# A constant tile of a transformer-layer kernel made 64 bytes larger, so that everything laid out behind it moves by 64 bytes

## The chip, the core and the metric

The kernel runs on one core of one Trainium2 chip. The time is in microseconds of device time for one execution, the median of several runs. The core has a matrix engine (TensorE, "PE" in the profile, with its weight loads shown apart as "PEld"), VectorE ("DVE"), ScalarE ("ACT"), GpSimd ("POOL") and SyncE ("SP"), which here issues the DMAs. Data lives on the chip in SBUF, 128 partitions with one address range that all partitions share; a tile takes the same byte range in every partition. Matmul results go to PSUM.

## The reference

One layer of a streaming encoder, for 512 tokens of width 2048, in fp32:

```
mod = silu(c) @ w_ada + b_ada                        # six vectors: sh1 sc1 g1 sh2 sc2 g2
h = rms_norm(x, norm1_g) * (1 + sc1) + sh1
proj = h @ w_in                                      # 8 gated-recurrence heads and 8 attention heads of 128
mixed = concat(hgrn2(...), stick_breaking(...)) @ w_out
x = x + g1 * mixed
h = rms_norm(x, norm2_g) * (1 + sc2) + sh2
gate, up = split(h @ w_ffn_in)                       # 2048 -> 2 * 5632
x = x + g2 * ((silu(gate) * up) @ w_ffn_out)         # 5632 -> 2048
```

## The kernel before

All of it is one function, `trunk`. The projections are kept at fp32 accuracy by splitting each operand in two parts, a rounded one (`hi`, type float32r) and the rest (`lo`), and summing three matmuls: hi by hi, hi by lo, lo by hi. A weight block comes in by DMA into one of four `raw` buffers; `split` (lines 211 to 222) then has ScalarE write its `hi` part (line 220) and VectorE its `lo` part (line 221). There are three `hi` and three `lo` buffers, used in turn.

The stages, in order: a first product with the raw `x` (tiles `st`), the projections of the attention heads (`sbp`, 384 columns a matmul) with the attention itself beside them, those of the recurrence heads (`hgf`, `hgq`, `hgg`, 512 columns), the output projection (`wo`, 512 columns), the first feed-forward product (`ffA`, `ffB`, `ffC`, 256 columns) and the second (`foA`, `foB`, `foC`, 512 columns). The rows of the modulation `w_ada` are multiplied on VectorE in between (line 180).

In every one of these matmuls one operand is stationary: it is loaded into the array as 128 columns of 4 bytes, 512 bytes of each partition. The other is moving: 256, 384 or 512 columns stream past. Both are read from SBUF.

The first feed-forward product is the longest stage. It does 42 turns `f`, from 2 to 43; each has seven block products (a scheme that needs seven products where eight are usual), named by their weights `ff_1` to `ff_7`. A product is 24 matmuls: 8 blocks of the contraction, for each of which the `hi` weights meet the `hi` and the `lo` part of the activations and the `lo` weights meet the `hi` part. The weights are stationary; the activations `opA`, `opD`, `opB`, `opC` are moving. In this stage `split` takes, at every fourth call, a spare pair of buffers in place of the usual three (lines 214 to 215): `hi2` and `lo2`, allocated in the pool `tp` on the right-hand side. The profile calls weights in the spare pair `ff_1hi`, `ff_1lo` and so on, with an i or an o behind, and weights in the usual buffers `ff_1h`, `ff_1l`. In the last stage every fourth call takes a pair inside the place of `hlo` instead, on the left.

**The layout.** SBUF is given out from both ends. Pools on the left side begin at low addresses and follow one another in the order in which they are opened: `const`, `wp` (raw, hi, lo), `hp` (the two large operand tiles `hhi` and `hlo`, whose place `opB` and `opC` take later), then the pools of the stages. Pools with `side="right"` are laid from the top downwards: `x` and `x1`, later `tp` and `rp` (with the spare pair), later `T2` and `O`. A slot is rounded up to a multiple of 32 bytes. `lead`, the tile of the diff, holds two partial sums of the first modulation row; of its columns only the first two are ever used (lines 291 and 293). It is the fifth tile of `const`, behind `cond`, `small`, `ones` and `epsb`.

The places that follow from this, as bytes from the start of a partition, and what is left of each over a multiple of 256:

| tile | side | byte | over a multiple of 256 |
|---|---|---|---|
| `cond`, `ones`, ahead of `lead` | left | 384, 9216 | 128, 0 |
| raw buffers | left | 11040, 19232, 27424, 35616 | 32 |
| hi buffers | left | 43808, 47904, 52000 | 32 |
| lo buffers | left | 56096, 60192, 64288 | 32 |
| `hhi`, later `opB` | left | 68384 | 32 |
| `hlo`, later `opC` | left | 101152 | 32 |
| `opA` (later `opsA`), `opD` | left | 133920, 166688 | 32 |
| spare pair `hi2`, `lo2` | right | 213984, 218080 | 224 |

Blocks inside these tiles are 512 bytes or a multiple of it apart, so that every operand of a matmul begins as far over a multiple of 256 as its tile does.

Of the kernel before, what the change touches and what calls it, by code (L numbers as in the profile page):

```python
# [10 lines left out]
F32 = mybir.dt.float32  # L11
# [6 lines left out]
P = 128  # L18
# [111 lines left out]
def trunk(ctx, tc, a):  # L130
# [5 lines left out]
    const = ctx.enter_context(tc.tile_pool(name="const", bufs=1))  # L136
# [20 lines left out]
    one = ones[:, 0:1]  # L157
    epsb = const.tile([P, 1], F32, name="epsb")
    G.memset(epsb, EPS)
    lead = const.tile([P, 2], F32, name="lead")  # L160
    left = [KT] * 6
    mod = const.tile([P, 96], F32, name="mod")
    gain1 = const.tile([P, KT], F32, name="gain1")
# [1179 lines left out]
```

## Time and profile before

| | |
|---|---|
| median of 3 runs | 2311.63 us (2308.95 to 2312.49) |
| the profiled execution | 2309.45 us, of which the span of the instructions is 2307.6 us |
| PE busy | 2253.1 us, 98% of the span |
| PEld busy | 2049.8 us, 89% |
| DVE busy | 1919.5 us, 83% |
| ACT busy | 1160.1 us, 50% |
| DMA queue | 53.0% of 16 engines' time, 435.42 MB |
| mean granted clock of TensorE | 0.995 |

The profile comes from one execution. A row of a group gives the source line, the engine, the operation, output and inputs, the shapes, the count, then the busy time in us and the mean of one in ns. Nearly all matmuls stand at line 93, in a helper. A matmul's own duration is longer than the distance from one matmul to the next, since several are in flight; the cost of one in a stream is read from the distance between starts. The chain of waits follows the work that ended last, from the last instruction back.

### The profile page before, as it was taken

Reading aid. Unit: us, or ns where it says so; the run is one execution under the profiler, and the core shown is the slowest. Engines: PE = TensorE matmul, PEld = TensorE weight load, DVE = VectorE, ACT = ScalarE, POOL = GpSimd, SP = SyncE. Lnnn points to the kernel's source line nnn. Section 1 sums busy time; section 2 is a strip of 40 time slices with the busy share of each in tenths; the row PEclk is TensorE's granted clock in tenths of the full one; section 3 lists DMA queues with packets and bytes.
Section 4 is the critical chain, followed back from the end, with each engine's and each line's share of the span. In section 5 each row is a group of like instructions: output and inputs, shape, how many; then the busy total and the mean of one; then the engine's idle time right before and its main releaser. Section 6 shows DMA issues by size and latency. Waiting matters only on the chain.

```text
span 2307.6 us, 35720 instructions
## 1 busy us (share of the span) xinstructions
PE 2253.1 (98%) x14171; PEld 2049.8 (89%) x14171; DVE 1919.5 (83%) x2570; ACT 1160.1 (50%) x2011; POOL 10.7 (0%) x25
## 2 busy tenths in 40 slices
PE   8999899999999999989999999999999999999998
PEld 6899799888888788989999999999999978878776
DVE  8887779999887864699899988888888777888888
ACT  4326666565656422654445444454545545454443
POOL 0000000000000000000000000000000000000000
PEclk9999999999999999999999999999999999999999
DMA  9886446843322486336555534454544486654553
GB/s 368 314 319 225 166 153 230 305 170 126 110 92 76 155 294 209 111 114 238 206 203 197 209 133 165 142 174 142 174 142 157 177 343 237 219 178 142 183 204 87
DMA packets 114978, 437.69 MB, mean 190 GB/s; under 512 B 9822, under 2 KB 58236, under 8 KB 76796
## 3 DMA queue, kind: packets, MB, share of 16 engines
q1 hardware_dynamic: 114812, 435.42, 53.0%
q8 instruction: 111, 1.82, 0.3%
q14 instruction: 55, 0.45, 0.1%
HBM read 386.61 MB, written 48.77 MB: 189 GB/s over the span
## 4 chain that ended last, share of the span: by engine, by line
PE 79%; DVE 11%; DMA 4%; ACT 3%; issue 3%; SPq 0%; DVEq 0%; ACTq 0%
PE ffA L93 17%; PE ffC L93 9%; PE foA L93 8%; PE sbp L93 8%; PE wo L93 7%; PE ffB L93 4%; PE foC L93 4%; PE st L93 4%; PE hgf L93 4%; PE hgq L93 3%; PE hgg L93 3%; PE foB L93 1%; DVE ada L180 1%; PE l L93 1%; DMA opd<-fhi 1%
## 5 line engine op out<-in xcount | busy, mean ns | idle before, releaser
L180 DVE SCALAR_TENSOR_TENSOR ada<-ada,cond 128x2048 f32<-128x2048 f32 x95 | 216.9, 2286 | 49.0 <-DMA ada<-in_w_ada 49.0
L93 PE MATMUL ffA<-opD,ff_3h 128*128 128x256 f32 x512 | 93.6, 283 | 0.8 <-ACT u L1008 0.8
L93 PE MATMUL ffA<-opB,ff_6h 128*128 128x256 f32 x512 | 93.6, 283 | 0.2 <-ACT a L1008 0.2
L93 PE MATMUL ffC<-opB,ff_7h 128*128 128x256 f32 x512 | 93.5, 283 | 0.0
L93 PE MATMUL ffC<-opC,ff_4h 128*128 128x256 f32 x496 | 90.8, 284 | 0.4 <-ACT c L1008 0.3
L93 PE MATMUL ffB<-opA,ff_2h 128*128 128x256 f32 x496 | 91.3, 284 | 0.0
L93 PE MATMUL ffA<-opC,ff_5h 128*128 128x256 f32 x496 | 90.6, 283 | 0.0
L93 PE MATMUL ffA<-opA,ff_1h 128*128 128x256 f32 x496 | 90.6, 283 | 0.0
L1082 ACT CAST fhi<-forms 128x512 fp32r<-128x512 f32 (+1 forms) x63 | 43.6, 692 | 90.6 <-DMA opd<-fhi 74.1
L93 PEld LDWEIGHTS ffA<-opD,ff_3h 128*128 128x128 f32 x512 | 79.8, 192 | 1.0 <-ACT u L1008 1.0
L93 PEld LDWEIGHTS ffA<-opB,ff_6h 128*128 128x128 f32 x512 | 79.7, 192 | 0.4 <-ACT a L1008 0.4
L93 PEld LDWEIGHTS ffC<-opB,ff_7h 128*128 128x128 f32 x512 | 79.8, 192 | 0.0
L93 PEld LDWEIGHTS ffC<-opC,ff_4h 128*128 128x128 f32 x496 | 77.2, 192 | 0.8 <-ACT c L1008 0.8
L93 PEld LDWEIGHTS ffB<-opA,ff_2h 128*128 128x128 f32 x496 | 77.7, 193 | 0.1
L93 PEld LDWEIGHTS ffA<-opC,ff_5h 128*128 128x128 f32 x496 | 77.3, 192 | 0.0
L93 PEld LDWEIGHTS ffA<-opA,ff_1h 128*128 128x128 f32 x496 | 77.3, 192 | 0.0
L1083 DVE TENSOR_TENSOR forms<-forms,fhi 128x512 fp32r<-128x512 f32 (+1 forms) x63 | 49.0, 778 | 31.0 <-ACT fhi L1082 30.6
L93 PE MATMUL ffA<-opD,ff_3l 128*128 128x256 f32 x256 | 72.5, 283 | 0.0
L93 PE MATMUL ffC<-opB,ff_7l 128*128 128x256 f32 x256 | 72.4, 283 | 0.0
L93 PE MATMUL ffA<-opB,ff_6l 128*128 128x256 f32 x256 | 72.4, 283 | 0.0
L93 PE MATMUL ffB<-opA,ff_2l 128*128 128x256 f32 x248 | 70.3, 284 | 0.0
L93 PE MATMUL ffA<-opA,ff_1l 128*128 128x256 f32 x248 | 70.2, 283 | 0.0
(1644 smaller groups left out, 7759.3 us busy)
## 6 DMA issues: line engine op xcount, KB each, us to landing
ada<-in_w_ada SPq DMA_DIRECT2D x95, 1024.0 KB, 5.0
wfo<-in_w_fo SPq DMA_DIRECT2D x16, 1024.0 KB, 6.0
yraw<-in_w_fo SPq DMA_DIRECT2D x16, 1024.0 KB, 5.1
fix<-in_w_fix SPq DMA_DIRECT2D x14, 1024.0 KB, 5.7
opsA<-opd SPq DMA_DIRECT2D x12, 1024.0 KB, 4.9
opd<-forms SPq DMA_DIRECT2D x44, 256.0 KB, 3.7
opd<-fhi SPq DMA_DIRECT2D x42, 256.0 KB, 4.2
opd<-forms SPq DMA_DIRECT2D x22, 384.0 KB, 6.7
```

The source lines that it names most:

```text
L93: self.engine.matmul(out, lhsT, rhs, **kw)
L180: V.scalar_tensor_tensor(w, w, 1.0, row, op0=ALU.mult, op1=ALU.mult, accum_out=col)
L1082: S.copy(hi, R[:, q])
L1083: V.tensor_sub(R[:, q].bitcast(F32R), R[:, q], hi.bitcast(F32))
```

## The change

The tile `lead` gets 18 columns in place of 2. It takes 96 bytes a partition in place of 32.

```
-    lead = const.tile([P, 2], F32, name="lead")
+    lead = const.tile([P, 18], F32, name="lead")
```

Nothing else is edited. The program has the same instructions on every engine, in the same order and with the same waits. Each tile on the left side behind `lead` begins 64 bytes higher: raw, hi, lo, `hhi`, `hlo` and the operands are 96 bytes over a multiple of 256, where they were 32. The tiles ahead of `lead`, all tiles on the right side, with the spare pair among them, PSUM and HBM are where they were.

## The prediction

> **What bounds the kernel now.** I read the page first, then the groups of instructions, then a table of stretches, and last the chain of waits in order of time. The page's busy times and the shares of the chain:
>
> ```profile
> PE 2253.1 (98%) x14171; PEld 2049.8 (89%) x14171; DVE 1919.5 (83%) x2570; ACT 1160.1 (50%) x2011; POOL 10.7 (0%) x25
> ...
> PE 79%; DVE 11%; DMA 4%; ACT 3%; issue 3%; SPq 0%; DVEq 0%; ACTq 0%
> ```
>
> TensorE is busy for 98% of the span and makes 79% of the chain, so the time is mostly a count of matmuls times what one costs in a stream. A change that moves no instruction can only act through the length of single operations, and it must act on matmuls to be seen. So I ask whether any operation's length depends on where its operands lie, and this program holds a test of that: in the first feed-forward stage most weights lie in the left buffers, one product in four in the spare pair on the right. The groups:
>
> ```profile
> L93 PE MATMUL ffC<-opB,ff_7h 128*128 128x256 f32 x512 | 93.5, 283 | 0.0
> ...
> L93 PE MATMUL ffA<-opA,ff_1hi 128*128 128x256 f32 x176 | 32.7, 288 | 6.2 <-ACT sg L1104 6.2
> L93 PE MATMUL ffA<-opC,ff_5hi 128*128 128x256 f32 x176 | 30.5, 276 | 0.0
> ...
> L93 PE MATMUL ffC<-opB,ff_7hi 128*128 128x256 f32 x160 | 27.7, 276 | 0.0
> ```
>
> The same shape with the same moving tile `opB` takes 283 ns with left weights and 276 ns with spare ones. (The 288 of `ff_1hi` holds a first wait.) In the chain of waits, in a stretch where PE is never stopped, the distance itself is seen. A turn of `f` runs 1, 2, 6, 7, 5, 4, 3, and columns are start, length, work:
>
> ```profile
> 1230.45 5.60 PE ffA L93 x48
> 1236.05 2.88 PE ffB L93 x24
> 1238.93 2.88 PE ffA L93 x24
> 1241.81 2.72 PE ffC L93 x24
> 1244.53 2.88 PE ffA L93 x24
> 1247.41 2.88 PE ffC L93 x24
> ```
>
> A product of 24 matmuls takes 2.88 us, 120.0 ns for each, or 2.72 us, 113.3 ns each, once in four (the 5.60 is one of either kind). The changes from one to the other fall on the spare products:
>
> ```profile
> 1173.37 0.28 PE L93 MATMUL ffA<-opD,ff_3l 128*128 128x256 f32 x1
> 1173.49 0.39 PE L93 MATMUL ffA<-opA,ff_1hi 128*128 128x256 f32 x2
> ...
> 1176.21 0.40 PE L93 MATMUL ffB<-opA,ff_2h 128*128 128x256 f32 x2
> ```
>
> `ff_1` from the spare pair lasts from 1173.49 to 1176.21, 2.72 us. So the length of a matmul does depend on where its weights lie, by 6.7 ns. Nothing else in those two products differs: `ff_1hi` and the `ff_2h` that follows it both stream `opA`.
>
> **What the 6.7 ns look like.** Three widths of the same kind of matmul, all with left operands on both sides:
>
> ```profile
> 423.41 4.16 PE sbp L93 x24
> ...
> 1855.96 5.44 PE foA L93 x24
> ```
>
> 384 columns take 173.3 ns, 512 take 226.7 ns, 256 take 120.0. Each step of 128 columns adds 53.3 ns, 0.417 ns a column, so that 256 columns alone are 106.7 ns. What is left over is 13.3 ns at all three widths with left weights, and 6.7 ns with spare weights. A fixed extra that does not grow with the width belongs to an event that happens once per matmul, and 6.7 ns are 16 columns, or 64 bytes of a partition. That is the size of a unit in which both operands could be fetched, and it is also the size of the shift.
>
> **The change part by part.** VectorE and ScalarE first. The same split, into the spare pair and into a left buffer:
>
> ```profile
> L220 ACT CAST ff_1hi<-wg10r x1: 1047/1047/1047, 1165.0 to 1165.0; 128x1024 fp32r<-128x1024 f32 x1
> L221 DVE TENSOR_TENSOR ff_1lo<-wg10r,ff_1hi x1: 1226/1226/1226, 1166.1 to 1166.1; 128x1024 fp32r<-128x1024 f32 x1
> ...
> L220 ACT CAST ff_1h<-wg11r x1: 1052/1052/1052, 1185.0 to 1185.0; 128x1024 fp32r<-128x1024 f32 x1
> L221 DVE TENSOR_TENSOR ff_1l<-wg11r,ff_1h x1: 1224/1224/1224, 1186.1 to 1186.1; 128x1024 fp32r<-128x1024 f32 x1
> ```
>
> 1047 against 1052 and 1226 against 1224 ns: neither engine cares. I cost them at nothing; with VectorE at 83% and ScalarE at 50% there is room besides. The wider `lead` itself costs nothing, since the same two columns are written and read.
>
> DMAs next. They make 4% of the chain, 92 us. All loads of weights go to the left side and keep their size; I cost them at nothing, and even 1% on all of these would be 0.9 us either way. [...]
>
> The matmuls carry the sum. For them the position of the operands can count in two ways, by itself or against the other operand. Look at the distances. Left weights and left moving tiles lie a multiple of 256 bytes apart, before and after, since both shift. The spare pair lies 224 over a multiple of 256 and the moving tiles 32: they are 192 apart modulo 256, an odd number of 64-byte units. After the change the moving tiles are at 96, and the distance is 128, an even number of units, like the left weights' distance of nothing. **If what matters is whether weights and moving operand run through the same half of a 128-byte pattern at the same time**, all the rows above follow: left against left meets once in each matmul, waits one unit of 16 columns (6.7 ns), and then runs out of step, so that the price is the same at every width; spare against left never meets. I take this as likeliest because the extra is one unit, occurs once, and does not depend on the width. Counting the units that the weights touch explains nothing: 512 bytes from 32 and 512 bytes from 224 cross equally many boundaries of 64, 128 or 256 bytes.
>
> What follows is a loss, and only for the spare products, which would go from 2.72 to 2.88 us. Their number comes from the seven groups of `hi` weights in the spare pair, of which the first, the third and the last stand above: four with 176 matmuls and three with 160 are 1184, and at 16 a product that is 74 products. 74 times 0.16 us is 11.8 us. How much of it reaches the end depends on whether PE sets the pace:
>
> ```profile
> 1005.00:1150.00 145.00, 139.90 (x1152) 139.25 (x1152) 135.06 (x154) 71.36 (x105) 0.00 (x0) 0.98 0.55 195
> 1150.00:1845.00 695.00, 693.99 (x5859) 693.59 (x5860) 587.06 (x662) 348.59 (x509) 0.00 (x0) 1.00 0.48 168
> ```
>
> (Columns: stretch, its length, busy us of PE, PEld, DVE, ACT, POOL, clock, DMA share, GB/s.) From 1150 to 1845 PE is busy for 693.99 of 695 us, and every lost ns counts: 35 turns with 7/4 spare products each are 61, or 9.8 us. From 1005 to 1150 PE has 5 us idle and the chain runs through DMAs and VectorE; the other 13 products cost between nothing and 2.1 us there. I take 1.2, a bit over half, as PE is still 96% busy: 11.0 us in all, with bounds of 9.8 and 11.8. All other stages keep their distance of nothing and their times. Sum against the profiled execution's own time, 2309.45 us (span 2307.6 and 1.85 around it): 2309.45 + 11.0 = **2320.5 us**. That execution lies 2.2 us under the median of 2311.63; with that and the bounds the likeliest case spans 2318 to 2325.
>
> **Rivals.** *No change.* What sets the 6.7 ns may be something that the shift leaves alone: the region (the spare pair lies above 208 thousand bytes, all left weights below 69 thousand), or a pattern longer than 128 bytes, in which the new distance of 128 is as good as 192. For it: all rows fix only one fast and one slow case. Against it: the extra of just 16 columns points to a short pattern, and weights at 68384 (`hhi`, in the `sbp` row above) or 133920 (`opsA`, in the `foA` row above) cost the same 13.3 ns as those at 43808, so region does not show among them. Time: 2309.5 to 2312, the profiled execution to the median. [...]
>
> *Faster.* The weights' position may count by itself. Modulo 128 the spare pair stands at 96 and left tiles at 32; after the change all left tiles stand at 96 too. If a start at 96 is what saves 6.7 ns, the other 220 of the 294 products gain 0.16 us each: 35 us, 2274. If matmuls of other stages gain as well, there are 1536 of 384 columns, 4104 of 512 and 480 more of 256 in the program, at 6.7 ns some 41 us more, 2233; but there VectorE and DMAs make part of the chain, and I take 60 us in all, 2249. VectorE would not stop the gain in the long stage: 587 us of busy time fit in 695 − 29. For it: one and the same position fits the fast rows. Against it: no count of boundaries tells 32 from 96. It decides if absolute position rules, whatever the distance.
>
> *Much slower.* A start at 96 for the moving operands may cost a second 6.7 ns everywhere: 13176 matmuls in the program, 88 us, 2397. No row shows a moving operand elsewhere than at 32, so it can't be excluded.
>
> **How the numbers follow.** Likeliest case 0.36, no change 0.34, faster 0.25 (most of it with all stages), much slower 0.05. The forecast is 2320.5 us. No two of the first three can be left out of a range that should hold 8 times in 10, so it goes from 2242, under the faster case at 2249, to 2326, over the likeliest one's top. About 0.2%, 4.6 us, is what a measurement of this kernel can tell from no change. Faster 0.25, same 0.34, slower 0.41.
>
> **What would show it.** In the profile after, groups `ff_1hi` to `ff_7hi` at 283 ns and no 2.72 left in the chain: the likeliest case. Those at 276 and `ff_7h` at 283: no change. `ff_7h` at 276 and `foA` under 5.44: faster. If `ff_7h` or `foA` grow, the moving operand counts by itself. In each case VectorE's 1.22 us and ScalarE's 1.05 us should stay; if they move, the argument is wrong at its first step.

## The result, and the profile after

| | before | after |
|---|---|---|
| median | 2311.63 us (2308.95 to 2312.49, 5 runs) | 2318.41 us (2314.87 to 2321.05, 5 runs) |
| ratio to before | | 1.0035, 95% interval 1.0024 to 1.0045 |
| span of the profiled execution | 2307.6 us | 2316.3 us |
| long stage (first `ffA` matmul to first `foB` matmul) | 842.1 us | 849.3 us |

The kernel is 0.35% slower, and the forecast of 2320.5 us is 2.1 us above the median. The medians lie 6.8 us apart, where the forecast added 11.0 us. The page of the kernel after, busy times and shares of the chain:

```profile
PE 2262.7 (98%) x14171; PEld 2059.2 (89%) x14171; DVE 1920.3 (83%) x2570; ACT 1162.2 (50%) x2011; POOL 10.7 (0%) x25
PE 80%; DVE 11%; DMA 3%; issue 3%; ACT 3%; SPq 0%; DVEq 0%; ACTq 0%
```

PE is busy for 9.6 us more with the same 14171 matmuls; VectorE and ScalarE stay within 2.1 us of theirs. The groups of the kernel after (source line, engine, operation, output and inputs, shapes, count, then busy us, mean ns of one, idle time before):

```profile
L93 PE MATMUL ffC<-opB,ff_7h 128*128 128x256 f32 x512 | 93.5, 283 | 0.0
L93 PE MATMUL ffA<-opA,ff_1hi 128*128 128x256 f32 x176 | 33.9, 293 | 6.2 <-ACT sg L1104 6.2
L93 PE MATMUL ffA<-opC,ff_5hi 128*128 128x256 f32 x176 | 31.7, 281 | 0.0
L93 PE MATMUL ffC<-opB,ff_7hi 128*128 128x256 f32 x160 | 28.9, 281 | 0.0
L221 DVE TENSOR_TENSOR ff_5lo<-ffS,ff_5hi 128x1024 fp32r<-128x1024 f32 x11 | 13.4, 1219 | 0.0
```

Left weights are as they were. Spare weights went from 276 to 281 ns, not to 283. VectorE's split takes the 1.22 us that it took before. The chain in order of time, the same place as before (start, length, work):

```profile
1239.24 2.88 PE ffB L93 x24
1242.12 2.88 PE ffA L93 x24
1245.00 2.84 PE ffC L93 x24
1247.84 2.88 PE ffA L93 x24
1250.72 2.88 PE ffC L93 x24
1253.60 5.72 PE ffA L93 x48
```

Where 2.72 us stood, 2.84 stands now: 118.3 ns a matmul in place of 113.3. The 5.72 is one product of each kind. 74 products by 0.12 us are 8.9 us, and the span grew by 8.7. The stretch with PE at work throughout:

```profile
1150.00:1845.00 695.00, 694.59 (x5809) 694.38 (x5807) 586.58 (x661) 346.78 (x503) 0.00 (x0) 1.00 0.48 166
```

PE is as busy as before and does 50 matmuls fewer in the same 695 us; by the chain, the dearer ones are the spare products. The long stage took 7.2 us more, where its 74 spare products by 0.12 us make 8.9, and the 61 of them from 1150 on make 7.3. The first stage took 0.8 us less, that of `sbp` 1.8 us more, the others within 0.4; experiments below with the same operand distances in `sbp` show 336.3 to 338.0 us for it, so that I do not put its part down to the change. Nor do I read anything into 8.7 lying so close to 8.9: the 8.7 holds that part.

### The profile page after: what moved, and what is told of

It is laid out like the page before. It is cut to its first block, busy times and chain, and to the rows that moved or that the text cites. A ratio compares the mean times of both kernels' runs of the same rounds, so it can differ in the third digit from the quotient of the medians.

```text
span 2316.3 us, 35720 instructions
## 1 busy us (share of the span) xinstructions
PE 2262.7 (98%) x14171; PEld 2059.2 (89%) x14171; DVE 1920.3 (83%) x2570; ACT 1162.2 (50%) x2011; POOL 10.7 (0%) x25
## 4 chain that ended last, share of the span: by engine, by line
PE 80%; DVE 11%; DMA 3%; issue 3%; ACT 3%; SPq 0%; DVEq 0%; ACTq 0%
PE ffA L93 19%; PE ffC L93 9%; PE foA L93 8%; PE sbp L93 8%; PE wo L93 7%; PE ffB L93 5%; PE foC L93 4%; PE st L93 4%; PE hgf L93 4%; PE hgq L93 3%; PE hgg L93 3%; PE foB L93 1%; DVE ada L180 1%; PE l L93 1%; PE sbo L93 1%
## 5 line engine op out<-in xcount | busy, mean ns | idle before, releaser
L93 PE MATMUL ffA<-opC,ff_5l 128*128 128x256 f32 x248 | 70.2, 283 | 0.0
```

What stands on the lines that cost most here:

```text
L93: self.engine.matmul(out, lhsT, rhs, **kw)
```

## The experiments

In the texts and tables, **the distance** is the start of the stationary operand less that of the moving one, modulo 256 bytes. The price of a matmul is the mean distance in time from one matmul's start to the next; those over 9 ns from the median (stops, missing records) are left out. Edits shift tiles with pads, a pool that holds one unused tile. Except in the last two kernels, every engine does the work of before in the same order; in the last two, ScalarE and VectorE take part of theirs in another order, which is the same in both. All prices, in ns, of the first feed-forward product (256 columns) and of two stages with 512 columns; in `fo` the roles are swapped, the weights being the moving side. The `fo` column leaves out the pair inside the place of `hlo`, which moves together with the operands and so has the distance 0 in every kernel:

| kernel | left weights: distance, ns | spare pair: distance, ns | `wo`: distance, ns | `fo`: distance, ns | long stage, us | time, us |
|---|---|---|---|---|---|---|
| before | 0: 120.0 | 192: 113.4 | 0: 226.9 | 0: 227.2 | 842.1 | 2311.63 |
| after | 0: 120.0 | 128: 118.3 | 0: 226.9 | 0: 227.2 | 849.3 | 2318.41 |
| both sides moved | 0: 120.0 | 192: 113.5 | 0: 226.9 | 0: 227.3 | 843.2 | 2311.85 |
| lead 256 larger | 0: 120.0 | 192: 113.5 | 0: 226.9 | 0: 227.2 | 840.5 | 2308.93 |
| gap 64 | 192: 117.8 | 128: 118.9 | 192: 229.0 | 64: 233.3 | 840.6 | 2321.81 |
| gap 128 | 128: 118.6 | 64: 113.8 | 128: 231.3 | 128: 232.7 | 841.6 | 2325.87 |
| weights on the right | 192: 117.8 | 192: 117.8 | 192: 229.2 | 64: 233.3 | 841.3 | 2321.76 |
| gap 192 | 64: 117.6 | 0: 119.9 | 64: 233.3 | 192: 229.9 | 848.2 | 2331.47 |
| gap 32 | 224: 116.7 | 160: 119.9 | 224: 233.3 | 32: 233.4 | 843.9 | 2328.86 |
| gap 96 | 160: 119.9 | 96: 117.5 | 160: 233.3 | 96: 234.0 | 849.8 | 2336.83 |
| gap 64, spare moved | 192: 114.3 | 0: 119.9 | 192: 229.2 | 64: 233.3 | 840.1 | 2319.44 |
| gap 192, spare moved | 64: 113.8 | 128: 118.3 | 64: 233.3 | 192: 229.6 | 842.5 | 2326.93 |
| shifted stage, two `fhi` | 192: 113.8 | 0: 120.0 | 0: 226.9 | 0: 227.2 | 822.1 | 2288.14 |
| two `fhi` alone | 0: 120.0 | 192: 113.4 | 0: 226.9 | 0: 227.2 | 839.0 | 2307.41 |

### Is it the distance, or each operand's own place?

Both sides are moved: the left tiles by 64 bytes as in the change, and the spare pair by 192 the other way, which brings its distance back to 192 modulo 256.

```
-    lead = const.tile([P, 2], F32, name="lead")
+    lead = const.tile([P, 18], F32, name="lead")
...
     xctx = ctx.enter_context(ExitStack())
+    ctx.enter_context(tc.tile_pool(name="rpadp", bufs=1, side="right")).tile([P, 48], F32, name="rpad")
```

> The change (all left tiles 64 bytes higher) and a pad of 192 bytes on the right side, which puts every right tile 192 bytes lower. Modulo 256 the spare pair has then moved by the same 64 as the moving operands: spare weights 32, moving 96, distance 192 as before the change. Instructions, order and waits are unchanged. Theory (the distance between weights and moving operand sets the price): the spare products go back to 2.72 us, 113.3 ns a matmul, the left ones stay at 2.88, and the time goes back to that of the kernel before, 2308 to 2313 us. Rival (each operand's own place has its price, and the prices add: spare weights at 224 save 6.7 ns against 32, a moving operand at 96 costs 5 ns more than at 32): spare weights are now at 32 as left ones were, so a spare matmul takes 106.7 + 13.3 + 5 = 125 ns, 3.00 us a product, and the time is 74 times 0.28, some 21 us, over the kernel before: about 2332.

Measured: 2311.85 us, ratio 1.0004 (0.9995 to 1.0014). The groups of this kernel:

```profile
L93 PE MATMUL ffC<-opB,ff_7h 128*128 128x256 f32 x512 | 93.5, 283 | 0.0
L93 PE MATMUL ffC<-opB,ff_7hi 128*128 128x256 f32 x160 | 27.7, 276 | 0.0
```

Both rows are those of before to the last digit, though every operand here has a new place. The loss of the change is undone by restoring the distance.

The second run makes `lead` larger by 256 bytes, which moves all left tiles and leaves all distances modulo 256.

```
-    lead = const.tile([P, 2], F32, name="lead")
+    lead = const.tile([P, 66], F32, name="lead")
```

> The tile of the change made 256 bytes larger in place of 64: every left tile 256 bytes higher. Theory (distance, modulo 256): nothing moves by its measure; spare products 2.72 us, left 2.88, time as the kernel before, 2308 to 2313 us. If the pattern is longer than 256 bytes the spare pair's price changes, up to 12 us more or a few us less. Rival (a larger tile, or the higher place of the left side in itself, costs time, and not the distance): 2314 to 2322 us as after the change or more.

Measured: 2308.93 us, ratio 0.9992 (0.9983 to 1.0001), the same prices. For the spare pair, the only weights whose distance moved by 256 bytes here, the price is the same again, and a larger `lead` costs nothing by itself.

### Does an odd number of 64-byte units always save?

The prediction's rule says so. A pad between the weight buffers and the operand tiles changes the distance of the left weights, which all stages use.

```
     xctx = ctx.enter_context(ExitStack())
+    ctx.enter_context(tc.tile_pool(name="padp", bufs=1)).tile([P, 16], F32, name="pad")
```

> The kernel before with a pad of 64 bytes between the weight buffers and the operand tiles: left weights stay at 32 over a multiple of 256, moving operands go to 96, the spare pair stays at 224. Theory (distance): left weights in the first feed-forward stage are now 192 from their moving operand, so their products go from 2.88 to 2.72 us (220 of them, 35 us), the spare ones are at 128 and go to 2.84 us as after the change (9 us back); hgf, hgq, hgg and wo go from 226.7 to 220.0 ns. In st, sbp and the last stage the roles are swapped and the distance is 64, of which no row tells the price. Net 2270 to 2290 us. Rival (own places, added): the moving operand at 96 costs 5 ns everywhere with weights at 32: left products 3.00 us, 232 ns at 512 columns where the moving one is the operand tile, 2340 us and more.

Measured: 2321.81 us, ratio 1.0040 (1.0025 to 1.0056): a miss, and on the other side. Groups, then the chain in the last stage:

```profile
L93 PE MATMUL ffC<-opB,ff_7h 128*128 128x256 f32 x512 | 91.8, 279 | 0.0
L93 PE MATMUL ffC<-opB,ff_7hi 128*128 128x256 f32 x160 | 29.0, 282 | 0.0
```

```profile
1909.38 5.60 PE foA L93 x24
1914.98 5.54 PE foC L93 x24
```

(In the second line only 12 of the 24 use the usual buffers; the other 12 are of the pair inside the place of `hlo`.) Left weights at the distance 192, an odd number of units, fell only to 117.8 ns, where the spare pair at the same distance had 113.4. At 512 columns the price went up: 5.60 us for 24, 233.3 ns, where before has 5.44. A gap of 128 bytes (`[P, 32]` in the same place) went the same way:

> As the run with the pad of 64, with 128 bytes: left weights 32, moving operands 160, spare pair 224. Theory (distance): left weights are 128 from the moving operand in the long stage, the distance of the spare pair after the change, and take 118.3 ns a matmul in place of 120.0, 2.84 us a product: 220 times 0.04 is 9 us less. In every other stage the distance is 128 too, whichever operand is stationary, and 512 columns go from 226.7 to about 225 ns. The spare pair is 64 away: price unknown, between 106.7 and 120 ns. Net 2290 to 2312 us. Rival (own places): a moving operand at 160 has a price that no row shows, but it is the same for left and spare weights, so that the spare products stay 6.7 ns under the left ones.

Measured: 2325.87 us, ratio 1.0062 (1.0049 to 1.0076). 512 columns at the distance 128 took 231 to 233 ns, not 225: a miss too. In the first feed-forward product left weights at 128 took 118.6, about what the spare pair has at 128 in the kernel after (118.3): so far the price goes with the distance. But the spare pair, now at 64, took 113.8:

```profile
L93 PE MATMUL ffC<-opB,ff_7h 128*128 128x256 f32 x512 | 92.5, 281 | 0.0
L93 PE MATMUL ffC<-opB,ff_7hi 128*128 128x256 f32 x160 | 27.7, 276 | 0.0
```

Twice the spare pair had the low price, and left weights not. So the next question was whether its place was what mattered.

### Is it the place of the spare pair?

All six `hi` and `lo` buffers move to the right side, so that all weights have the distance 192.

```
     xctx = ctx.enter_context(ExitStack())
+    wq = ctx.enter_context(tc.tile_pool(name="wq", bufs=3, side="right"))
...
-            hi = wp.tile(shape, F32R, tag="hi", name=name + "h")
-            lo = wp.tile(shape, F32R, tag="lo", name=name + "l")
+            hi = wq.tile(shape, F32R, tag="hi", name=name + "h")
+            lo = wq.tile(shape, F32R, tag="lo", name=name + "l")
```

(The first block's two tiles move likewise.)

> The kernel before, with the six hi and lo buffers of the weights taken from the left side and laid at the top of the right side (bytes 204768 to 229344, 224 over a multiple of 256); the operand tiles stay 32 over one, 24576 bytes lower, the spare pair stays at 224, also 24576 bytes lower (189408). All weights are then 192 from the moving operand in the long stage, as the spare pair is before the change. Same instructions, order and waits. The run with the pad of 64 had left weights at that distance at 117.8 ns, and not at the 113.4 of the spare pair. Theory (distance together with the place: weights above the moving operands in SBUF are cheaper than weights below them): ffA to ffC 113.3 ns for all weights, 35 us less there; hgf, hgq, hgg, wo have the same distance and roles and go from 226.7 towards 220 ns; st, sbp and the last stage have the operand tiles stationary at a distance of 64 and go to some 233 ns as with the pad of 64, 9 to 12 us back. Net 2275 to 2295. Rival (distance, and a spare pair is cheap because it is one pair among others, wherever it lies): main weights 117.8 ns, 512 columns 229 to 233, as with the pad of 64, 2315 to 2325.

Measured: 2321.76 us, ratio 1.0045 (1.0028 to 1.0062). Groups:

```profile
L93 PE MATMUL ffC<-opB,ff_7h 128*128 128x256 f32 x512 | 91.9, 280 | 0.0
L93 PE MATMUL ffC<-opB,ff_7hi 128*128 128x256 f32 x160 | 28.7, 280 | 0.0
```

Neither kind has the low price now, and the spare pair rose from 113.4 to 117.8 ns, at the distance that it has in the kernel before. Place and spare pair as such are out. What differs between its products here and those of before is what ran ahead of them: there a product at 120.0 ns, here one at 117.8.

Three other gaps (192, 32 and 96 bytes: `[P, 48]`, `[P, 8]`, `[P, 24]`) were to map the distance.

> As the run with the pad of 64 between weight buffers and operand tiles, with 192 bytes: weights 32, moving operands 224, spare pair 224. Theory (distance): the spare pair's distance is now nothing, as the left weights' is before the change, and its matmuls take 120.0 ns; left weights are 64 away in the long stage and in hg and wo, which go to some 233 ns at 512 columns as st did at a distance of 64; st and the last stage are 192 away and take some 229 to 230, as hg and wo did. Rival (the roles and not the distance tell 229 from 233): st and the last stage stay at 233, hg and wo at 229. Rival (own places): the spare pair stays cheap, 113 ns.

> Pad of 32 bytes: weights 32, operands 64, spare pair 224; distances 224 for left weights in the long stage, 160 for the spare pair, 32 in st and the last stage. Theory (a unit of 64 bytes that either coincides or not): half a unit away still coincides in part, prices between those at the neighbours: left 118 to 120 ns, spare 113 to 118.5, 512 columns 227 to 233. Rival (moving operands that start on a multiple of 64 bytes need one unit less, which none of the runs so far had): 6.7 ns less everywhere, 113 ns and 220 ns.

> Pad of 96 bytes: weights 32, operands 128, spare pair 224; distances 160 for left weights in the long stage, 96 for the spare pair, 96 in st and the last stage. Theory (unit of 64 bytes): left 117.8 to 118.6, spare 113 to 118.5, 512 columns 229 to 233. Rival (operand tiles on a multiple of 64 need one unit less): 6.7 ns less than with pads of 64 and 128, wherever the operand tiles are moving.

Measured: 2331.47, 2328.86 and 2336.83 us, a single run each. The prices expected for the gap of 192 came; of those for 32 and 96 only that of the spare pair with the gap of 96 lies in its range. With the gap of 192 the spare pair comes to the distance 0 and takes 119.9 ns, as left weights do there. At 512 columns 64 and 192 changed their prices together with their stages (`wo` 233.3 and `fo` 229.9, where the gap of 64 has 229.0 and 233.3), so that there the distance decides and not the stage. The distance is not all, though: the pair inside the place of `hlo`, always at the distance 0, took 227.5 ns on average in the kernel before and 230.1 with the gap of 192. There the first four steps of its streams of twelve took 232 to 233 ns and the last 227, which fits an after-effect of the dearer matmuls ahead that wears off. Of the distances tried, 0 is the cheapest at 512 columns (227), then 192 (229 to 230), then 128 (231 to 233), and the others 233 to 234. The gap of 32 refutes a rival in which a moving operand on a multiple of 64 saves a unit: that asked for 113 and 220 ns, and 116.7 (left), 119.9 (spare) and, in `wo`, 233.3 came.

### Two rhythms at one distance?

The rows so far fit if a stream at the distance 192 has two steady rhythms, 113.4 and 117.8 ns, and the product ahead decides which of them holds. At 192 the low one had been seen only behind products at 120.0; at 64, only behind products at 118.6. Two kernels keep the left weights of the gaps of 64 and of 192 and change what runs ahead of them alone: a pad of 128 bytes on the right moves the spare pair.

```
     xctx = ctx.enter_context(ExitStack())
+    ctx.enter_context(tc.tile_pool(name="padp", bufs=1)).tile([P, 16], F32, name="pad")
+    ctx.enter_context(tc.tile_pool(name="rpadp", bufs=1, side="right")).tile([P, 32], F32, name="rpad")
```

(and `[P, 48]` for `pad` in the second)

> As the 64-byte gap, but the spare pair is also moved, by 128 bytes, so that its distance to the moving tiles is 0 instead of 128; the left weights keep the distance 192. The 64-byte gap gave 117.8 ns for left weights at 192, while spare weights at 192 had given 113.4. Theory: there are two steady rhythms at the distance 192 (about 113.4 and 117.8 ns a matmul at 256 columns), and which one holds is set by the product before; 113.4 was seen only where a product at 120.0 (distance 0) came before. So the left products behind each spare product go to 113.4 ns, the spare ones to 120.0; the long stage falls from 842 to some 805 to 815 us; with some 20 us more in the other stages, as the 64-byte gap showed, the time is about 2290. Rival: left weights cost 117.8 at a distance of 192 whatever came before; left 117.8, spare 120.0, the long stage about 842 to 846, the time 2320 to 2327.

> As the 192-byte gap, with the spare pair moved by 128 bytes too: left weights stay at the distance 64, the spare pair goes from 0 to 128. At 64, left weights behind a spare product at 120.0 took 117.6 ns; in the kernel with the 128-byte gap a spare pair at 64 behind products of 118.5 took 113.8. Theory of two rhythms: the left products, now behind a spare product at 118.5, go to 113.4 to 113.8 ns; the long stage falls to some 810 to 815 us, the time to about 2295. Rival (the product before does not matter): left stays at 117.6, spare 118.5, long stage 845 to 848, time about 2330.

Measured: 2319.44 us, ratio 1.0047 (1.0029 to 1.0065), and 2326.93 us in a single run. The prices came as the two rhythms say; the times did not. Groups of the first, where left weights fell from the 279 ns that they have with the same gap and the old spare pair:

```profile
L93 PE MATMUL ffC<-opB,ff_7h 128*128 128x256 f32 x512 | 88.8, 276 | 0.0
L93 PE MATMUL ffC<-opB,ff_7hi 128*128 128x256 f32 x160 | 29.2, 283 | 0.0
```

Both rhythms stand in this one execution. The matmuls in order of time (start, length, work; the last bracket is idle time), first in the second product behind a spare one, with no stop between, then right behind a stop:

```profile
1243.92 0.28 PE L93 MATMUL ffB<-opA,ff_2l 128*128 128x256 f32 x1
...
1244.26 0.28 PE L93 MATMUL ffB<-opA,ff_2l 128*128 128x256 f32 x1
...
1244.60 0.28 PE L93 MATMUL ffB<-opA,ff_2l 128*128 128x256 f32 x1
...
1244.94 0.28 PE L93 MATMUL ffB<-opA,ff_2l 128*128 128x256 f32 x1
```

```profile
1277.95 0.50 PE L93 MATMUL ffA<-opD,ff_3h 128*128 128x256 f32 x2 [1.31 <-ACT u L1008]
...
1278.64 0.28 PE L93 MATMUL ffA<-opD,ff_3l 128*128 128x256 f32 x1
...
1279.35 0.28 PE L93 MATMUL ffA<-opD,ff_3l 128*128 128x256 f32 x1
...
1280.06 0.28 PE L93 MATMUL ffA<-opD,ff_3l 128*128 128x256 f32 x1
```

Every third matmul uses an `l` tile. The rows above are 0.34 us apart, three matmuls of 113.3 ns each; those below the first are 0.71 us apart, six matmuls of 118 ns each, at the same distance. Counted over the whole stage, left products that follow a spare one (120 ns) directly, with no stop or missing record in it, ran at 113 ns in 57 cases of 58; those that began right behind a stop, over 250 ns after the last matmul's start, ran at 118 in 17 of 18. At the distance 64 it is the other way about: behind a spare product at 120 (the gap of 192) 65 of 66 ran at 118; behind one at 118.3 (the gap of 192 with the spare pair moved) 58 of 59 ran at 113, and there 15 of 19 ran at the low price right behind a stop too.

**Why the time did not fall.** 220 left products of 24 by 3.5 ns (117.8 to 114.3) are 18 us, less 2 for the spare ones (118.9 to 119.9), yet the long stage went from 840.6 to 840.1. In the table of stretches PE is busy for 684.69 us where it had 693.99 before:

```profile
1150.00:1845.00 695.00, 684.69 (x5864) 680.70 (x5863) 588.41 (x666) 345.40 (x509) 0.00 (x0) 1.00 0.49 169
```

The waits in that stage, from 1020 to 1850, first of the kernel before, then of this one (engine, line, releaser: us in total, times, longest):

```profile
ACT fhi L1082 <- DMA opd<-fhi: 74.1, 40, 3.8
...
DVE forms L1083 <- ACT fhi L1082: 30.6, 27, 2.2
```

```profile
ACT fhi L1082 <- DMA opd<-fhi: 103.5, 41, 5.4
...
DVE forms L1083 <- ACT fhi L1082: 39.9, 29, 2.9
```

`fhi` (line 1082) rounds the operands of the second product; it has one buffer, which a DMA must empty before ScalarE may write it again. In the order of the program, splits and other copies stand behind it on ScalarE and begin after it, as `u` does below, and VectorE's subtraction on line 1083 waits in turn, 39.9 us in all. The chain of this kernel goes through that DMA:

```profile
1270.79 0.44 DVE forms L1074
...
1271.25 0.84 ACT fhi L1082
...
1272.11 4.82 DMA opd<-fhi
...
1277.01 0.62 ACT fhi L1082
1277.63 0.28 ACT u L1008
```

After it comes the stop of 1.31 us at 1277.95 above. The copy `u` of a finished product, which stands behind `fhi` on ScalarE and began at 1277.63 as `fhi` ended, released PE. The stop also costs a second time: the rhythm begins again at 118. With other gaps too the stage took more than the prices alone make. With the gap of 32 they would make it 6 us shorter than before; it took 1.8 us longer, with 87.4 us of that wait. With the gap of 192 they would make it 1 us shorter; it took 6.1 us longer, with 69.5 us of that wait, less than before. So the account above is shown for this run, and not for every gap.

### With that chain relieved

The layout of the last run, for the first feed-forward product only: `opA` to `opD` are placed 64 bytes higher inside enlarged slots, the other stages keep the distance 0, the spare pair has 0 too, and `fhi` gets two buffers.

```
+    ctx.enter_context(tc.tile_pool(name="rpadp", bufs=1, side="right")).tile([P, 32], F32, name="rpad")
...
-    hlo = hp.tile([P, KT, T], F32R, tag="hlo", name="hlo")
+    hlo = hp.tile([P, 8240], F32R, tag="hlo", name="hlo")[:, 48:8240].rearrange("p (k t) -> p k t", k=16)
...
-    late = hp.tile([P, 2, HALF, 2, HT], F32R, tag="hhi", name="opB")
+    late = hp.tile([P, 8208], F32R, tag="hhi", name="opB")[:, 16:8208].rearrange("p (a k b t) -> p a k b t", a=2, k=8, b=2)
...
-                hi = tp.tile([P, b - a, HT], F32R, tag="fhi", name=f"fhi{f}_{a}", bufs=1)
+                hi = tp.tile([P, b - a, HT], F32R, tag="fhi", name=f"fhi{f}_{a}", bufs=2)
```

(the other tiles of these slots in the same way)

> The layout of the run with left weights at 192 and the spare pair at 0, but only in the first feed-forward product: all other stages keep their distance of 0 and their times. And fhi, in which ScalarE rounds the seven operands of the second product before a DMA takes them to HBM, gets two buffers in place of one. In that earlier run left products took 113.4 ns a matmul in a good part of the long stage, but the stage stayed at 840 us: ScalarE's fhi waited 90 us for the DMA that empties the one buffer, VectorE's subtraction behind it 39 us for ScalarE, weights came late, PE stood still, and after each stop the left products began again at 117.8. Theory (two rhythms, and this chain as what took the gain back): with two buffers the stops go, left products stay at 113.4 once a spare product at 120 has passed, the long stage falls to 812 to 822 us, and the time to 2282 to 2292. Rival (VectorE, busy for 92% of the time from 1200 to 1300, or the weight loads set the pace): the long stage stays at 835 to 842 us, the time 2303 to 2309, not to be told from before.

Measured: 2288.14 us, ratio 0.9900 (0.9885 to 0.9915). The chain, where 2.88 is now a spare product, then the stretch and the wait on the buffer from 1020 to 1850:

```profile
1251.36 2.72 PE ffB L93 x24
1254.08 2.72 PE ffA L93 x24
1256.80 2.72 PE ffC L93 x24
1259.53 2.88 PE ffA L93 x24
```

```profile
1150.00:1845.00 695.00, 694.39 (x5949) 690.87 (x5948) 600.23 (x676) 355.16 (x513) 0.00 (x0) 1.00 0.49 179
```

```profile
ACT fhi L1082 <- DMA opd<-fhi: 17.8, 17, 2.8
```

The waits of 103.5 us went to 17.8. PE is busy throughout, and does 5949 matmuls where before had 5859, though the stretch already holds some of the next stage here. 5280 left matmuls by 6.2 ns are 33 us won, 1776 spare ones by 6.6 are 12 us lost; 21 should remain, and the long stage fell by 20.0. VectorE, at 600 of 695 us, did not stop it. The control has the second buffer alone, in the layout of before:

> The kernel before with two buffers for fhi and nothing else: left weights at a distance of 0, the spare pair at 192. It tells which part of the faster version does what. Theory (the distances give the gain, the second buffer only lets it through): PE is busy for 827 of the 830 us from 1020 to 1850 already, so the buffer has at most 3 us to give; pitches stay at 120.0 and 113.4, the long stage at 839 to 843 us, the time at 2306 to 2312. Rival (the second buffer is what made the faster version fast): the long stage falls below 830 us, the time below 2300.

Measured: 2307.41 us, ratio 0.9988 (0.9979 to 0.9997). Its long stage takes 839.0 us, 3.1 less than before, about the idle time that PE had there (2.9 us from 1020 to 1850); but three kernels with the prices of before and one buffer also differ by 2.7 us in that stage (840.5 to 843.2). The prices are those of before. Between the last two kernels the layout alone differs, and the long stage by 16.9 us: the distances give the gain, and the buffer lets it through. Two ends are open. With the buffer came another order of work on ScalarE and VectorE, and no run tells the two apart; and the layout without the second buffer was tried in that stage only together with a worse layout in the others.

## Why the prediction was right, and where it was off

**Only lengths of operations can change, and only the matmuls' matter: right.** VectorE and ScalarE are indifferent to the shift: VectorE's split into the spare pair takes 1219 ns in both kernels, ScalarE's 1052 and 1049 ns (medians for `ff_5`), and PE carries the difference.

**The distance between weights and moving operand decides: right.** The forecast took this from one row of fast products and one of slow ones; moving both sides settled it. With that the rivals fall. *Faster* and *much slower* rest on an operand's own place, and all operands moved at an unchanged price (120.0 and 113.5 ns, where before has 120.0 and 113.4). *No change* needed the region or a longer pattern: in the kernel after the spare pair has not moved and its price has, 118.3 ns a matmul in place of 113.4, where of its two operands only the moving one had a new place.

**The term of 0.16 us for each spare product: too large.** The step that failed is that the distance 128 is like the distance 0, since both are an even number of units. It measured 118.3 ns and not 120.0, so 0.12 us a product; 74 of them make 8.9 us in place of 11.8. At 256 columns 128 has a price of its own, in the kernel after and with the gap of 128. (The bounds of that case, 9.8 and 11.8 us on 2309.45, and 2.2 us for the median, make 2319 to 2323.5, a little less than the 2318 to 2325 that it was given.)

**The rule behind that term: only part of the truth.** "Spare against left never meets" would have made every stream at an odd number of units cheap. At 512 columns all other distances tried are dearer (229.0 to 234.0 ns) than the distance 0 (226.9 to 227.3), and at 256 the distances 64 (113.8 and 117.6) and 192 (113.4 and 117.8) have two prices. That both operands are fetched in units of 64 bytes, and that one waits a unit for the other, was a conjecture of mine from the 6.7 ns; no run shows it. That the price at the distance 0 is one fixed extra at all three widths (13.3 ns of the 120.0, 13.6 of the 226.9) is a fact of that distance, and no other distance bears it out: over the 106.7 and 213.3 ns that 0.417 ns a column make, the gap of 128 has 11.9 ns at 256 columns and 18.0 at 512 (`wo`). So the loss was forecast by a rule that failed with the next gap tried (64 bytes) and at 512 columns. That its size came out near is in part luck: the rule made 128 equal to 0, and 128 only lies near it at 256 columns (118.3 against 120.0; at 512, 231.3 to 232.7 against 227). The case had been given a chance of 0.36, hardly more than no change.

**How much reaches the end: about right.** PE sets the pace in the long stage. Of 8.9 us, 7.2 appear there, at the lower of the two bounds scaled to 0.12 (7.3 for 61 products, 8.9 for 74). That the 13 products ahead of 1150 cost nothing is not shown by it: kernels with the prices of before differ by 2.7 us in that stage. The sum started from the profiled execution, 2.2 us under the median; by medians the change is 6.8 us, and from the median the forecast would have been 4.2 us too high and not 2.1. That part of the closeness is luck.

**A side remark that fell short.** Under the rival *faster* stood that VectorE's 587 us would not stop a gain in the long stage. VectorE did not, at 600 us in the fastest kernel, but its busy time alone could not tell: in the first kernel with left products at 113 nothing was gained in the long stage (840.1 us); 822.1 came with the second buffer.

**What stays open.** Why the prices are what they are, and how the rhythm of one product is handed to the next, no view shows. The two rhythms are shown as behaviour, at the distances 64 and 192 and at 256 columns. The after-effect at 512 columns is seen in averages alone.

## What to carry to other kernels

If one shape of matmul shows two lengths in one kernel, as 276 and 283 ns here, compare the SBUF addresses of its two operands modulo 256 bytes, and what ran just before; a resized constant at the low end of the layout can shift operands on its side against those on the other side in every stage behind it. Test such a theory by moving both operands together, and at every width that the kernel has, before a layout is chosen: what gains at 256 columns loses at 512 here (gap of 64, spare moved: left products 114.3 ns for 120.0, but `wo` 229.2 for 226.9 and `fo` 233.3 for 227.2). When cheaper matmuls gain nothing, look for single-buffered tiles that another engine waits for (`fhi` here: 103.5 us of waits, 17.8 with two buffers and the shifted stage), and not at busy shares alone.

## What the runs showed of the hardware that I had not expected

- The price of an fp32r matmul depends on the distance of its operands modulo 256 bytes, and on what ran ahead: 113.4 to 120.0 ns at 256 columns, 226.9 to 234.0 at 512.
- The best distance depends on the width: 0 is the cheapest tried at 512 columns (226.9 to 227.3 ns) and the dearest, with 160, at 256 (119.9 to 120.0).
- At 256 columns and the distances 64 and 192 two rhythms hold, 113.4 to 113.8 and 117.6 to 117.8 ns. What runs ahead picks one: at 192, 57 of 58 left products directly behind a spare one at 120 ran at 113, and 17 of 18 right behind a stop at 118. It lasts: in the chain of the shifted stage three left products of 2.72 us stand one behind the other, up to the next spare one.
- A stop of PE can therefore cost more than its length: at the distance 192, 17 of 18 products that began right behind one ran 4.4 ns a matmul slower.
